# A transformer block in float32r halves: matmul tiles placed at other offsets within 128 bytes

## The chip, the cores and the metric

One NeuronCore of a Trainium2 chip runs the whole program in one launch. The metric is the device time of that core in microseconds (us). The engines named below are TensorE (PE; its loads of the stationary operand are listed apart, as PEld), VectorE (DVE), ScalarE (ACT), GpSimd (POOL) and SyncE (SP), which issues most transfers.

## What is computed

The reference is one block over 256 tokens of width 2048: a modulated norm, a mixer (three attention branches beside a gated linear recurrence), a second modulated norm, and a layer of 16384 small experts, 16 picked for each of 8 heads. Cut to what matters here:

```python
mod = jax.nn.silu(c) @ ada_w + ada_b                    # six vectors of 2048
h = rms_norm(x, norm_mix_g) * (1 + sc1) + sh1
x = x + gt1 * hybrid_mixer(h, w_in, w_out, ...)         # z = h @ w_in ; ... ; y @ w_out
h = rms_norm(x, norm_ffn_g) * (1 + sc2) + sh2
q = h @ peer_wq                                         # scores, top 16 of each head -> e, g
act = gelu(einsum('td,thkd->thk', h, down[e])) * g
x = x + gt2 * einsum('thk,thkd->td', act, up[e])
```

The kernel does the expert layer densely: all of `down` times the tokens, gelu, a gate that is zero for experts that were not picked, then all of `up`.

## The kernel before

Every large product runs in three matmuls. A float32 operand is split into two float32r halves, `h` (high) and `l` (the rest): ScalarE casts the high half and VectorE subtracts it from the source (`split`, L197 and L198). Then `mm3` issues high times high (L346), token high times weight low (L347) and token low times weight high (L348) into the same sums. The stationary operand is a slice of 128 token columns; the moving operand is 512 columns of weights. `mm_sub` does this for the two chunks of 128 rows in one part of the stream and for both halves of the tokens (`tb`), so one part costs 12 matmuls, in the order L346, L347, L348, again and again.

Weights come as one stream. SyncE loads 1 MB raw tiles (`raw`, four buffers); `next_part` takes 1024 columns of one at a time, splits it into a buffer `wh` and a buffer `wl`, and `get` hands the pair to the matmuls. There are three buffers of each in the pool `wp`; among the first 52 parts, two of each five use two more in the pool `xp`. The tokens are `xH` and `xL` (16 KB a partition each), written three times: after the first norm, by the mixer's output, after the second norm. In the last stage the tokens' place is taken by the gated activations `ah` and `al` (four buffers each).

The stages, by the names of the sums that the matmuls write: `f`, `a`, `r`, `xg` (the mixer's input projections, to about 350 us, mixed with attention and recurrence), `y` (output projection), `wq` (queries of the experts), then `d` (expert blocks down) and `u` (up). The first 14 `d` blocks run from 480 to 960 us beside the search and the gate build; then six rounds of `u` alone; then two `u` blocks and one `d` block in turn to about 2020 us; then the last `u` blocks. A block of `d` is 96 of these matmuls, a block of `u` is 48.

The allocator puts every tile at a multiple of 32 bytes. Within 128 bytes, the built program of before has `xH` and `xL` at 64, `wh` and `wl` of the pool `wp` at 32, those of the pool `xp` at 96, `ah` and `al` at 32. All slices of these tiles start at multiples of 512 bytes from the tile's start, so each tile's offset holds for all its slices.

Of the kernel before, what the change touches and what calls it, by code (L numbers as in the profile page):

```python
# [15 lines left out]
P = 128  # L16
D = 2048
S = 256
# [47 lines left out]
def kernel(  # L66
# [48 lines left out]
    cs = cp.tile([P, NDC], F32, name="cs")  # L115
    xH = cp.tile([P, NDC, S], F32R, name="xH")
    xL = cp.tile([P, NDC, S], F32R, name="xL")
    ident = con[:, C_ID:C_ID + P]
# [8 lines left out]

# [1 line left out]
    items = []  # L129
# [47 lines left out]
    def load(most=RAWB):  # L177
        """Loads the stream ahead, as far as the rings allow."""
        while pos["load"] < len(items):
            it = items[pos["load"]]  # L180
            if len(raws) >= most:
                return
            t = wp.tile([P, D], F32, tag="raw", bufs=RAWB, name="raw")
            if it[0] == "ada":
                nc.sync.dma_start(t, ada_w[ada_w.shape[0] - NDC + it[1]])
            elif it[0] == "adp":
                nc.sync.dma_start(t, ada_p[it[1]])
            elif it[0] == "cmp":
                nc.sync.dma_start(t, cmp_w[it[1]][:, it[2] * D:(it[2] + 1) * D])
            else:  # L190
                n = it[2] * it[3]
                nc.sync.dma_start(t[:, 0:n], it[1])
            raws.append(t)
            pos["load"] += 1
# [5 lines left out]
    def ada_load():  # L200
        """Loads ahead, as far as the rings allow."""
        n = pos["adl"]
        if n < ada_w.shape[0] - NDC:
            own = n >= 2 * NDC or n < ADO and n % (ADAB + ADA1) < ADAB
            if sum(o == own for o, _ in avs) < (ADAB if own else ADA1):
                if own:
                    t = vp.tile([P, D], F32, tag="av", bufs=ADAB, name="av")
                else:
                    t = xp.tile([P, D], F32, tag="av1", bufs=ADA1, name="av1")
                nc.sync.dma_start(t, ada_w[n])  # L210
                avs.append((own, t))
                pos["adl"] += 1
                return True
        return False

    def ada(m):
        """One chunk of a modulation vector: rows of the turned weights times the conditioning."""
        t = avs.pop(0)[1]
# [5 lines left out]
    def ada_close(seg, k, n):  # L224
        """The biases; where it scales, one plus it, times the norm's gain."""
        m = mod[:, seg, k:k + n]
# [7 lines left out]
    def bg(r):  # L234
        """A share r of a chunk of the modulation vectors that VectorE makes beside the rest."""
        bgn[1] += r
# [13 lines left out]
    def adp_item():  # L250
        """A chunk of the rows of one modulation vector, in four column groups of the array."""
        i = items[pos["take"]][1]
# [9 lines left out]
        if k == NDC - 1:  # L262
            seg = PSEG[i // NDC]
            rw = wp.tile([P, 512], F32, tag="adr", bufs=1, name="adr")
            A.copy(rw, adp.pop("ps"))
# [7 lines left out]
    def next_part():  # L273
        """Emits the next part of the stream; False at its end."""
        if pos["take"] >= (pos["end"] or len(items)):
# [16 lines left out]
        pool, tag, bufs = (xp, "1", 2) if pos["n"] <= XPN and pos["n"] % 5 >= 3 else (wp, "", AHEAD + 1)  # L292
        wh = pool.tile([P, 2, 512], F32R, tag="wh" + tag, bufs=bufs, name="wh")
        wl = pool.tile([P, 2, 512], F32R, tag="wl" + tag, bufs=bufs, name="wl")
        fh, fl = wh.rearrange("p k n -> p (k n)"), wl.rearrange("p k n -> p (k n)")
# [18 lines left out]

# [1 line left out]
    jobs = []  # L316
# [13 lines left out]

    # steps per part of the stream, by the kind of work; the gate build's first steps go as fast as they may
    tk, wn = [0.0], [0]
# [7 lines left out]
    def finish(prio):  # L340
        """Runs the jobs up to that priority to their end."""
        while jobs and jobs[0][0] <= prio:
            step()
# [25 lines left out]
    def rsqrt(pool, ss, n, w, name, parts=P, bufs=2):  # L369
        """1/sqrt(ss/n + eps) of a few columns, by Newton's method from an integer first guess."""  # L370
        v = pool.tile([parts, w], F32, tag="rsv", bufs=bufs, name=f"rsv_{name}")
# [45 lines left out]

# [1 line left out]
    ea, e0, eq = ExitStack(), ExitStack(), ExitStack()  # L419
# [40 lines left out]
    def ada_first(n):  # L460
        """Chunks of the first two modulation vectors; the tokens' next two chunks when they are complete."""
        for _ in range(n):
# [10 lines left out]

    # two sets of four blocks, in turn over pieces of the width; the sums of the set that rests wait in SBUF
    sums = {"f": [], "a": []}
# [36 lines left out]
    def rest(b, name):  # L512
        """The rest of one of the first four blocks, added up in SBUF."""
        pst = [ps_x(f"{name}_{tb}") for tb in range(NT)]
# [17 lines left out]
    def mix(*gens, rate=0.0):  # L532
        """Steps of several pieces of work in turn."""
        gens = list(gens)
# [7 lines left out]

# [1 line left out]
    ap = ea.enter_context(tc.tile_pool(name="ap", bufs=1))  # L544
# [18 lines left out]
    vc = zp.tile([16, NG, HD], F32, name="vc")  # L563
    # the compressed branch borrows what the later branches fill
    win = oT.rearrange("p h t -> p (h t)").rearrange("p (a l g n) -> p a l g n", a=2, l=32, g=2)
# [3 lines left out]
    def table(i):  # L569
        """The rotation's tables with a norm's gains folded in."""  # L570
        gv = row[:, P * i:P * i + P]
# [8 lines left out]
    def rope(dst, src, nh, cos, sin, name):  # L580
        """dst = src*cos + swap(src)*sin over nh heads of 128."""
        b = tp1.tile([P, nh, 2, 64], F32, tag="ropeb", bufs=1, name=f"rb_{name}")
# [126 lines left out]

# [1 line left out]
    lw = rn.tile([P, 2, RB, P], F32, name="lw")  # L711
    G.dma_start(lw, lru_w)
    def recurrence(gr):
        n = RG
        if True:
# [4 lines left out]
            for c_ in range(n):  # L720
# [13 lines left out]
                A.activation(ta[:, c_], ta[:, c_], AF.Tanh, scale=spl[:, k:k + 1], bias=spl[:, k:k + 1])  # L734
            # d = 1/(1 + tanh) refined from (1 + exp)/2; decay 2d - 1; input sqrt(tanh) d (1 + ti) u
            d = xr[:, :, 0:S]
# [16 lines left out]

# [1 line left out]
    held = {}  # L755

    def scores(sp, g, tb):
        """Unnormed weights of the causal and the windowed branch, and their sums."""
        n = (tb + 1) * P
# [28 lines left out]
    def outputs(sp, g, tb):  # L788
        """The compressed branch's weights; all gated weights turned and times the values."""
        hs = slice(4 * g, 4 * g + 4)  # L790
# [56 lines left out]

# [1 line left out]
    def norm_stats(pool, rbs, o, name, pre=None):  # L849
# [174 lines left out]

# [1 line left out]
    ssr = yp.tile([P, NT], F32, name="ssr")  # L1026
# [22 lines left out]

# [1 line left out]
    bp = ctx.enter_context(tc.tile_pool(name="bp", bufs=1))  # L1051
# [19 lines left out]
    def ev_wq(j, pst):  # L1071
        """Scores of two heads; leaves them to the search."""
        res = []
# [19 lines left out]
    def search(j, tb, sc):  # L1093
        for k in range(4):
            top16(mv[:, tb, 4 * j + k], mi[:, tb, 4 * j + k], sc[:, k * P:(k + 1) * P], P, f"a{j}{tb}{k}")
            yield
        # both lists are sorted: rank (a, b) has (a + 1)(b + 1) - 1 before it, so only those under 16 can be picked
        cd = kq.tile([P, 2, NCD], F32, tag="cd", bufs=2, name=f"cd{j}{tb}")
# [14 lines left out]
    def picks(tb):  # L1113
        """From places in the candidate lists to expert rows, and the softmax; heads and picks on partitions."""
        hi = kq.tile([P, 2, PH, TOPK], U32, tag="hi", bufs=1, name=f"hi{tb}")
# [3 lines left out]
        V.tensor_copy(mf, mi[:, tb])  # L1119
        # place p of rank (a, b): a = max(p / 8 - 1, p / 4 - 6, 0), b = p - min(16 a, 8 a + 8, 4 a + 24)  # L1120
        V.tensor_scalar(hi[:, 0], pk[:, tb], 3, None, OP.logical_shift_right)
# [39 lines left out]
    def w_build():  # L1161
        """Gate weights by expert and token: per token the product of two one-hot tables."""
        stg, ohs, gas, wps = {}, {}, {}, {}
# [27 lines left out]

# [1 line left out]
    xTt, wts, actH, actL = {}, {}, {}, {}  # L1193
# [31 lines left out]
    def act(eb, pool):  # L1225
        t, w = xTt.pop(eb), wts.pop(eb)
        t4 = t.rearrange("p c (g t) -> p c g t", g=8)
        h = pool.tile([P, 4, S], F32R, tag="ah", bufs=4, name=f"ah{eb}")
        l = pool.tile([P, 4, S], F32R, tag="al", bufs=4, name=f"al{eb}")
# [182 lines left out]
```

## Time and profile before

| | before |
|---|---|
| median of 3 runs | 2092.45 us (2089.61 to 2093.78) |
| profiled execution: span from first to last instruction | 2090.6 us |
| mean granted TensorE clock in it | 0.986 of full speed |
| PE / PEld / DVE / ACT busy | 97% / 78% / 69% / 50% |
| instructions in the span | 24862 |
| HBM rate over the span | 243 GB/s |

The span lies inside the spread of the runs: what lies around it is smaller than the spread from run to run. Busy time of PE is the time in which at least one matmul is in the array; matmuls overlap, so it says that PE is hardly ever empty, and not how fast it goes. The page's mean of one matmul is from its start to the end of its drain, longer than the time from one start to the next, which I call the pitch.

### The profile page before, as it was taken

How to read it: one execution, taken by the hardware profiler on the slowest of the kernel's cores; microseconds unless marked ns; L12 is line 12 of the kernel's file. 1: busy time of each engine (PE TensorE's matmuls, PEld its weight loads, DVE VectorE, ACT ScalarE, POOL GpSimd, SP SyncE). 2: the span in 40 equal slices, each digit the busy share in tenths (PEclk: the TensorE clock that was granted, in tenths of full speed). 3: DMA queues.
4: the chain of work that ended last, by engine and by line, in shares of the span. 5: the costliest groups of instructions: out<-in, count | busy, mean ns of one | idle time of the engine just before them, and what ended most of it. 6: DMA issues, size and time to landing. Idle time of an engine off the chain costs nothing.

```text
span 2090.6 us, 24862 instructions
## 1 busy us (share of the span) xinstructions
PE 2025.0 (97%) x9434; PEld 1635.6 (78%) x9434; DVE 1449.4 (69%) x2149; ACT 1053.0 (50%) x1526; POOL 60.9 (3%) x95
## 2 busy tenths in 40 slices
PE   5999997999999999999999999999999999999998
PEld 4777664877888888887888888888888888888887
DVE  7888999887998666646667766665555555555566
ACT  3544676545456777854444444444444444444443
POOL 0000000000000000001000000000000000000000
PEclk8999998999999999999999999999999999999999
DMA  9897788994556666579777877765555565555563
GB/s 374 333 358 310 264 341 312 347 347 165 174 177 201 226 218 241 203 258 332 253 243 258 294 251 253 247 244 191 191 193 200 200 202 194 200 201 191 194 209 141
DMA packets 75849, 508.73 MB, mean 243 GB/s; under 512 B 8528, under 2 KB 9040, under 8 KB 20176
## 3 DMA queue, kind: packets, MB, share of 16 engines
q1 hardware_dynamic: 63792, 450.50, 60.5%
q0 software_dynamic: 11936, 56.63, 7.6%
q8 instruction: 74, 1.21, 0.2%
q14 instruction: 47, 0.39, 0.1%
HBM read 478.78 MB, written 28.31 MB: 243 GB/s over the span
## 4 chain that ended last, share of the span: by engine, by line
PE 86%; DVE 6%; issue 3%; DMA 3%; ACT 1%; POOL 0%; SPq 0%; DVEq 0%; POOLq 0%; ACTq 0%
PE d L348 11%; PE d L346 11%; PE d L347 11%; PE u L347 10%; PE u L348 10%; PE u L346 10%; PE w L1184 3%; DVE av L219 2%; DVE wl L198 2%; PE wq L346 1%; PE wq L347 1%; PE wq L348 1%; PE a L347 1%; PE a L348 1%; PE a L346 1%
## 5 line engine op out<-in xcount | busy, mean ns | idle before, releaser
L198 DVE TENSOR_TENSOR wl<-raw,wh 128x1024 fp32r<-128x1024 f32 x649 | 789.6, 1222 | 511.8 <-ACT wh L197 511.6
L197 ACT CAST wh<-raw 128x1024 fp32r<-128x1024 f32 x649 | 680.0, 1050 | 777.8 <-PE u L348 334.5
L346 PE MATMUL d<-wh,xH 128*128 128x512 f32 x1024 | 411.2, 402 | 0.0
L347 PE MATMUL d<-wl,xH 128*128 128x512 f32 x1024 | 405.1, 396 | 0.9 <-DVE wl L198 0.9
L348 PE MATMUL d<-wh,xL 128*128 128x512 f32 x1024 | 404.9, 395 | 0.0
L346 PE MATMUL u<-wh,ah 128*128 128x512 f32 x1024 | 402.1, 393 | 0.0
L347 PE MATMUL u<-wl,ah 128*128 128x512 f32 x1024 | 399.4, 390 | 1.3 <-DVE wl L198 1.2
L348 PE MATMUL u<-wh,al 128*128 128x512 f32 x1024 | 399.1, 390 | 0.0
L348 PEld LDWEIGHTS d<-wh,xL 128*128 128x128 f32 x1024 | 192.4, 188 | 45.8
L347 PEld LDWEIGHTS d<-wl,xH 128*128 128x128 f32 x1024 | 192.7, 188 | 43.9 <-DVE wl L198 1.3
L346 PEld LDWEIGHTS d<-wh,xH 128*128 128x128 f32 x1024 | 192.8, 188 | 42.6
L347 PEld LDWEIGHTS u<-wl,ah 128*128 128x128 f32 x1024 | 192.4, 188 | 41.8 <-DVE wl L198 3.0
L348 PEld LDWEIGHTS u<-wh,al 128*128 128x128 f32 x1024 | 192.2, 188 | 40.5
L346 PEld LDWEIGHTS u<-wh,ah 128*128 128x128 f32 x1024 | 192.3, 188 | 39.0
L219 DVE SCALAR_TENSOR_TENSOR av<-av,cb 128x2048 f32<-128x2048 f32 x64 | 146.0, 2285 | 5.4 <-DMA av<-in_ada_w_dram 5.4
L1168 DVE TENSOR_TENSOR oh<-con,idT 128x1024 f32<-128x1024 f32 x64 | 78.3, 1223 | 64.2 <-PE w L1184 64.2
L1189 ACT ACTIVATE oh<-oh,gT 128x128 f32<-128x128 f32 x256 | 83.7, 394 | 34.8 <-DVE oh L1168 34.5
L1256 DVE TENSOR_TENSOR acc<-acc,u 128x512 f32<-128x512 f32 x112 | 71.6, 681 | 0.0
L1184 PEld LDWEIGHTS w<-oh 128*128 128x128 f32 x512 | 65.5, 191 | 4.4
L1184 PE MATMUL w<-oh 128*128 128x128 f32 x512 | 66.6, 275 | 0.0
L346 PE MATMUL y<-wh,xH 128*128 128x512 f32 x128 | 52.1, 409 | 3.6 <-ACT xH L197 3.6
L346 PE MATMUL wq<-wh,xH 128*128 128x512 f32 x128 | 52.5, 410 | 2.5 <-ACT xH L197 2.5
(365 smaller groups left out, 2044.8 us busy)
## 6 DMA issues: line engine op xcount, KB each, us to landing
raw<-in_down_dram SPq DMA_DIRECT2D x128, 1024.0 KB, 5.0
raw<-in_up_dram SPq DMA_DIRECT2D x128, 1024.0 KB, 5.0
av<-in_ada_w_dram SPq DMA_DIRECT2D x64, 1024.0 KB, 7.1
raw<-in_w_a_dram SPq DMA_DIRECT2D x32, 1024.0 KB, 9.4
raw<-in_ada_p_dram SPq DMA_DIRECT2D x16, 1024.0 KB, 7.1
raw<-in_w_out_dram SPq DMA_DIRECT2D x16, 1024.0 KB, 7.9
raw<-in_wq_dram SPq DMA_DIRECT2D x16, 1024.0 KB, 5.0
wd<-stg POOLq DMA_DIRECT2D x8, 2048.0 KB, 8.0
```

Of the source, the lines that this page charges most:

```text
L197: A.copy(dst_h, src)
L198: V.tensor_tensor(dst_l, src, dst_h.bitcast(F32), OP.subtract)
L219: V.scalar_tensor_tensor(out=t, in0=t, scalar=1.0, in1=cb, op0=OP.mult, op1=OP.mult, accum_out=m)
L346: T.matmul(o, ah, bh, start=first, stop=False)
L347: T.matmul(o, ah, bl, start=False, stop=False)
L348: T.matmul(o, al, bh, start=False, stop=last)
L1168: V.tensor_tensor(oh, iota.unsqueeze(1).unsqueeze(1).to_broadcast([P, 4, 2, P]), idT[:, 4 * q:4 * q + 4].unsqueeze(3).to_broadcast([P, 4, ...
L1184: T.matmul(wps[p_][:, k * P:(k + 1) * P], oh[:, k, 1], oh[:, k, 0], start=True, stop=True)
L1189: A.activation(ohs[p_][:, k, 0], ohs[p_][:, k, 0], AF.Copy, scale=gT[:, t:t + 1])
L1256: V.tensor_tensor(a, a, pst[tb], OP.add)
```

## The change

`shifted` allocates a tile 32 elements (128 bytes) longer and uses it from 8 elements (32 bytes) times `by` on. It is applied to `xH` (by 3), `xL` (by 2), `ah` (by 1), and to each weight buffer by a count of the parts: `wh` by the count modulo 4, `wl` by the count divided by 4, modulo 4. `al` stays. The tile `adr` of 2 KB, used once, is now a buffer of the ring `zr` (two buffers), which makes room.

```diff
+    def shifted(pool, n, by, **kw):
+        return pool.tile([P, n + 32], F32R, **kw)[:, 8 * by:8 * by + n]
-    xH = cp.tile([P, NDC, S], F32R, name="xH")
-    xL = cp.tile([P, NDC, S], F32R, name="xL")
+    xH = shifted(cp, NDC * S, 3, name="xH").rearrange("p (k t) -> p k t", t=S)
+    xL = shifted(cp, NDC * S, 2, name="xL").rearrange("p (k t) -> p k t", t=S)
...
-            rw = wp.tile([P, 512], F32, tag="adr", bufs=1, name="adr")
+            rw = zrow(adpool[0], "adr")
...
-        wh = pool.tile([P, 2, 512], F32R, tag="wh" + tag, bufs=bufs, name="wh")
-        wl = pool.tile([P, 2, 512], F32R, tag="wl" + tag, bufs=bufs, name="wl")
+        turn = pos["n"] % 16
+        wh = shifted(pool, 1024, turn % 4, tag="wh" + tag, bufs=bufs, name="wh").rearrange("p (k n) -> p k n", k=2)
+        wl = shifted(pool, 1024, turn // 4, tag="wl" + tag, bufs=bufs, name="wl").rearrange("p (k n) -> p k n", k=2)
...
-        h = pool.tile([P, 4, S], F32R, tag="ah", bufs=4, name=f"ah{eb}")
+        h = shifted(pool, 4 * S, 1, tag="ah", bufs=4, name=f"ah{eb}").rearrange("p (k t) -> p k t", t=S)
```

Row by row, every engine has the same instructions in the same order before and after; only the name of the tile `adr` differs in two rows. The other tiles move by multiples of 128 bytes. With the base addresses of the built program of after, the offsets within 128 bytes become:

| tile | before | after |
|---|---|---|
| `xH` | 64 | 32 |
| `xL` | 64 | 0 |
| `ah` | 32 | 64 |
| `al` | 32 | 32 |
| `wh` (pool `wp`) | 32 | 32, 64, 96, 0 from part to part |
| `wl` (pool `wp`) | 32 | 32, 64, 96, 0, changing every four parts |

## Rows read from the trace of the kernel before

**Rows 1.** The page: busy time by engine, and the chain that ended last.
```profile
PE 2025.0 (97%) x9434; PEld 1635.6 (78%) x9434; DVE 1449.4 (69%) x2149; ACT 1053.0 (50%) x1526; POOL 60.9 (3%) x95
...
PE 86%; DVE 6%; issue 3%; DMA 3%; ACT 1%; POOL 0%; SPq 0%; DVEq 0%; POOLq 0%; ACTq 0%
```
**Rows 2.** Windows: busy PE, PEld, DVE, ACT, POOL (instructions); clock, DMA share, GB/s.
```profile
480.00:960.00 480.00, 479.13 (x2432) 399.83 (x2431) 343.00 (x694) 309.88 (x560) 18.01 (x31) 1.00 0.60 213
1160.00:2020.00 860.00, 859.07 (x3809) 701.14 (x3808) 500.10 (x511) 377.31 (x398) 16.32 (x20) 1.00 0.63 214
```
**Rows 3.** The page's costliest groups: matmuls of d and u, by operand.
```profile
L346 PE MATMUL d<-wh,xH 128*128 128x512 f32 x1024 | 411.2, 402 | 0.0
L347 PE MATMUL d<-wl,xH 128*128 128x512 f32 x1024 | 405.1, 396 | 0.9 <-DVE wl L198 0.9
...
L346 PE MATMUL u<-wh,ah 128*128 128x512 f32 x1024 | 402.1, 393 | 0.0
L347 PE MATMUL u<-wl,ah 128*128 128x512 f32 x1024 | 399.4, 390 | 1.3 <-DVE wl L198 1.2
...
L346 PE MATMUL wq<-wh,xH 128*128 128x512 f32 x128 | 52.5, 410 | 2.5 <-ACT xH L197 2.5
L346 PE MATMUL y<-wh,xH 128*128 128x512 f32 x128 | 52.1, 409 | 3.6 <-ACT xH L197 3.6
```
**Rows 4.** Timeline of PE (start us, us): ends of one undisturbed block of d.
```profile
1226.33 0.40 PE L348 MATMUL u<-wh,al 128*128 128x512 f32 x1
1226.57 0.39 PE L346 MATMUL d<-wh,xH 128*128 128x512 f32 x1
...
1248.96 0.39 PE L346 MATMUL u<-wh,ah 128*128 128x512 f32 x1
```
**Rows 5.** Stretch of u alone; only instructions of u; PE, PEld, DVE, ACT, clock.
```profile
1000.00:1150.00 150.00, 150.00 (x664) 124.19 (x663) 17.10 (x27) 0.00 (x0) 1.00 0.73 250
```
**Rows 6.** Timeline of PE: a part of u after four transposes.
```profile
1618.20 0.40 PE L347 MATMUL u<-wl,ah 128*128 128x512 f32 x1
...
1620.29 0.39 PE L347 MATMUL u<-wl,ah 128*128 128x512 f32 x1
```
**Rows 7.** Timeline of PE: a part of d after matmuls of the gate build.
```profile
689.37 0.40 PE L347 MATMUL d<-wl,xH 128*128 128x512 f32 x1
...
691.46 0.40 PE L347 MATMUL d<-wl,xH 128*128 128x512 f32 x1
```
**Rows 8.** Three us early in wq, after an idle stretch: clock, then timeline.
```profile
477.00:480.00 3.00, 3.00 (x8) 0.50 0.00 0
...
477.34 0.63 PE L347 MATMUL wq<-wl,xH 128*128 128x512 f32 x1
477.76 0.63 PE L346 MATMUL wq<-wh,xH 128*128 128x512 f32 x1
```
**Rows 9.** The recurrence's plain float32 matmuls: all (min/median/max ns), then seven in a row.
```profile
L730 PE MATMUL rp<-u,lw x32: 377/379/763, 245.5 to 333.1; 128*128 128x256 f32 x32
...
245.55 1.67 PE L730 MATMUL rp<-u,lw 128*128 128x256 f32 x7
```
**Rows 10.** Timeline of PE: first and last of 41 gate-logit matmuls in a row.
```profile
264.38 0.28 PE L346 MATMUL gl<-xH,wh 128*24 128x256 f32 x1
...
268.96 0.28 PE L347 MATMUL gl<-xL,wh 128*24 128x256 f32 x1
```
**Rows 11.** VectorE's subtraction (min/median/max ns), 40 to 160 us, then 960 to 2080 us.
```profile
L198 DVE TENSOR_TENSOR wl<-raw,wh x38: 1214/1220/1226, 44.1 to 154.6; 128x1024 fp32r<-128x1024 f32 x38
...
L198 DVE TENSOR_TENSOR wl<-raw,wh x399: 1216/1225/1227, 960.6 to 2077.7; 128x1024 fp32r<-128x1024 f32 x200
```
**Rows 12.** Timeline: the copy into adr, its four transposes, the next use of zr.
```profile
350.29 0.59 ACT L265 COPY adr<-adp 128x512 f32<-128x512 f32 x1 [0.82 <-PE adp L259]
...
351.20 0.60 PE L268 MATMUL adt<-con,adr 128*128 128x128 f32 x4
...
353.01 0.59 ACT L703 COPY zr_r<-xg 128x512 f32<-128x512 f32 x1 [2.13 <-PE xg L348]
```

## The prediction, made before the changed kernel ran

> **What bounds the kernel now.** I read the page first: PE is busy 97% of the span and holds 86% of the chain that ended last [rows 1]. Then I cut the span into stretches, because an average over stages says little. From 480 to 960 us PE has work for 479.13 of 480.00 us, from 1160 to 2020 us for 859.07 of 860.00 us, at full granted clock, while VectorE and ScalarE have room (500.10 and 377.31 us of the second stretch) and the transfers take 0.63 of the DMA engines [rows 2]. Two thirds of the kernel are therefore a queue of matmuls, and the time there is their number times their pitch, the time from one start to the next.
>
> The page's durations include the drain, so the reader should not take 402 ns for the cost of one. But they differ: matmuls of `d` last 402 and 396 ns, those of `u` 393 and 390 ns [rows 3], with the same shape, type and number. The timeline gives the pitch. A block of `d` starts at 1226.57 us and the first matmul behind its 96 starts at 1248.96 us: 22.39 / 96 = 233.2 ns [rows 4]. In 150 us of `u` alone, 664 matmuls touch the stretch, two of them as overlap at its start: 150 / 662 = 226.6 ns [rows 5]. What differs between the two is the stationary tile alone: `xH` and `xL` at offset 64, `ah` and `al` at 32, against weights at 32 in both. So the tile's place does matter, by some 6.6 ns a matmul, and it matters through the load that runs beside the moving operand: the last matmul of `u` before a block of `d` still has its own operands at 32 and 32, but the load of `xH` runs beside it, and it takes 1226.57 - 1226.33 = 0.24 us [rows 4].
>
> Two more views size what a better place could give. At half clock (granted 0.50), the same matmuls start 477.76 - 477.34 = 0.42 us apart [rows 8]. Plain float32 matmuls of 256 columns at full clock: seven in 1.67 us, the last with its drain of 0.379, so (1.67 - 0.379) / 6 = 215 ns [rows 9]. Half the pitch at half clock, 210 ns at this view's resolution, and this 215 agree; I take 216 ns as the floor of one such matmul at full clock (an estimate from these two rows). Over it `u` pays about 11 ns and `d` about 17. That is the whole stake: 17 ns times all matmuls paced by PE.
>
> **How a distance acts.** I describe a matmul by the distance, within 128 bytes, from the stationary tile loaded beside it to its weights. Before, it is 0 in all of `u` and 32 in all of the rest (32 one way for buffers of `wp`, the other way for those of `xp`, where the mixer's stages, mixed with other work, show no clean run to compare). A distance of 64 does not occur in a full matmul. The second thing that the timeline shows is that 226.6 is a settled state. After four transposes a part of `u` takes nine pitches from 1618.20 to 1620.29 us, 2.09 / 9 = 232.2 ns, although all its offsets are 32 [rows 6]. In `d` after an interruption nine pitches also take 691.46 - 689.37 = 2.09 us, 232.2 ns [rows 7]. Out of the settled state both distances cost the same; `u` gains its 5.6 ns by running long in one unchanged pattern.
>
> **The change part by part.** Instructions, their order, the queues and the transfers are the same, so nothing is added or moved on any engine. The costs are in four places.
>
> The adr tile: its ring neighbour `zr` is next written at 353.01 us, while the transposes that read adr end at 351.20 + 0.60 = 351.80 us [rows 12]. 1.2 us of cover, cost nothing; without cover it would be one copy of 0.59 us.
>
> Writes and reads of the shifted tiles by VectorE and ScalarE: VectorE's subtraction lasts 1220 ns (median) between 40 and 160 us, where two of five buffers lie at offset 96, and 1225 ns later, where all lie at 32, with minimum and maximum 12 ns apart at most [rows 11]. The offset costs them nothing. Were it 5 ns each, 649 of them would be 3 us of VectorE, hidden in its free 31% [rows 1].
>
> Matmuls that now lie at distance 32: `d`, `wq` and `y` have 3 x (1024 + 128 + 128) = 3840 that PE paces [rows 3]; a quarter of them go to each of the distances 0, 32, 64 and 32 the other way, since `wh` and `wl` walk through four offsets while `xH` and `xL` stand still. From part to part, every 12 matmuls, the distance changes, and inside a part L347 has another distance than L346 and L348. I therefore expect no settled state, and give each known distance the unsettled 232.2 ns.
>
> Matmuls now at distance 0: the 3072 of `u` [rows 3] lose their single pattern and also see all four distances. The remaining 864 (`f`, `a`, `r`, `xg`) share their stages with other work and are taken as unchanged; 1 ns on each would be 0.9 us.
>
> The unknown is X, the pitch at distance 64. From below, it cannot pass the floor of 216. From above, I continue the line of 226.6 at distance 0 and 233.2 at 32 to about 240 at 64 (an estimate from [rows 4, 5]). A mixture is in the trace: the gate logits run with all four distances in turn, 40 pitches from 264.38 to 268.96 us, 114.5 ns for 256 columns [rows 10]; doubled this is 229 ns, but their loads are 24 columns, not 128, so it is a low reading. Between 216 and 240 I take X equal to the unsettled 232.2, the row that full matmuls are nearest to. Then all distances cost 232.2:
> 3840 x (232.2 - 233.2) = -3.8 us; 3072 x (232.2 - 226.6) = +17.2 us; sum +13.4 us. The profiled span of 2090.6 would be 2104.0; the median of the runs lies 1.9 above that span, so 2092.45 + 13.4 = 2105.9, **2106 us**.
>
> A rule that speaks against any effect stands in the Trainium skill, page "TensorE: Matmul & The Clock Gate", Part 2, step 1: the array has separate read ports for the moving operand and for LDWEIGHTS, and loading the next weights "doesn't steal SBUF read bandwidth from the running matmul". By it the sum is 0 and the time 2092; this trace disagrees with it as far as `d` and `u` differ by 6.6 ns with nothing but the stationary tile exchanged [rows 4, 5].
>
> **The rivals.**
> *Faster: distance 64 is free of collisions.* If two streams collide by their place in 128 bytes, the farthest distance could reach the floor. With X = 216 the mean is (3 x 232.2 + 216) / 4 = 228.1: 3840 x -5.1 = -19.6, 3072 x +1.5 = +4.6, together -15 us, 2077 us. It decides at a mean pitch of (3840 x 233.2 + 3072 x 226.6) / 6912 = 230.3: below that the change gains. The 229 of the gate logits speaks for it, their short loads against it. If the changing offsets alone brought every matmul to the floor, it would be 3840 x -17.2 - 3072 x 10.6 = -99 us, 1994 us; nothing in the trace comes near 216 with 128 float32r columns loaded beside, and I give it 3 in 100.
> *Slower by more: distance 64 is worst.* With X = 240 the mean is 234.2: 3840 x 1.0 + 3072 x 7.6 = +27 us, 2119 us. For it speaks that 32 is worse than 0 when settled.
> *No change: the place in 128 bytes is not what makes the difference.* `xH` and `ah` also lie far apart in the partition, and `u` could be quick for that reason; then the shift does nothing, 2092 us. Against it: the unsettled runs show that the pitch of `u` is no property of its buffers.
>
> **How the numbers follow.** Forecast (all distances about 232): 0.40. Distance 64 worst: 0.17. Distance 64 free, or the mixture as quick as the gate logits: 0.27, the floor included. No change: 0.16. A measurement of this kernel cannot tell less than about 0.2%, 4 us, from nothing. Faster by more than that takes the third case with little of the first, 0.28; within 0.2% the fourth, 0.16; slower the first two, 0.56. The forecast's own range is 2098 to 2114; with the faster case at 2077 and the slower at 2119, and some room for X a little above the line, 8 in 10 lie between 2076 and 2124.
>
> **What the profile after would show.** Right: the pitch in `u` alone at about 232 instead of 226.6, with no long run of equal pitches, and a block of `d` at about 22.3 us instead of 22.39; so `u` and `d` move in opposite ways. VectorE's and ScalarE's durations, and the wait before the copy at 353.01 us, stay. In parts, by the count modulo 4, one in four should stand out if X is far from 232: its L346 and L348 are shorter (faster rival) or longer (slower rival). Wrong: `u` keeps 226.6, or `d` falls by more than 3 ns; then distances 0 and 64 average below what unsettled runs show, and my use of [rows 6, 7] as the price of a changing pattern is the step that failed.

## The result, and the profile after

The changed kernel is slower: a median of 2103.77 us (4 runs, 2101.69 to 2104.33) against 2093.11 us (4 runs, 2089.61 to 2094.94) of the kernel before on the same chip, a ratio of 1.0052 with a 95% interval of 1.0038 to 1.0067. The profiled span went from 2090.6 to 2101.5 us, at a mean granted clock of 0.985 after 0.986.

The page's busy times, answering to [rows 1]:

```profile
PE 2035.3 (97%) x9434; PEld 1636.0 (78%) x9434; DVE 1450.1 (69%) x2149; ACT 1051.0 (50%) x1526; POOL 60.9 (3%) x95
```

PE's busy time grew by 10.3 us, almost all of the span's 10.9; VectorE's and ScalarE's changed by 0.7 and -2.0 us. What is left of the span beside it is 66.2 us after 65.6. So no wait was added: the same 9434 matmuls took longer. The windows of the two long stretches, in the columns of [rows 2], say which:

```profile
480.00:960.00 480.00, 479.63 (x2437) 400.75 (x2436) 343.76 (x695) 310.27 (x560) 18.02 (x31) 1.00 0.61 214
1160.00:2020.00 860.00, 859.77 (x3784) 696.94 (x3783) 498.92 (x509) 372.52 (x394) 16.31 (x20) 1.00 0.63 214
```

In 480 us of `d` and the search, 2437 matmuls touch the window where 2432 did. In 860 us of mostly `u`, 3784 where 3809 did. One kind became a little quicker, the other slower. The page's groups agree (busy us, then mean ns of one; [rows 3] are those of before):

```profile
L351 PE MATMUL d<-wh,xH 128*128 128x512 f32 x1024 | 410.9, 401 | 0.0
L351 PE MATMUL u<-wh,ah 128*128 128x512 f32 x1024 | 407.1, 398 | 0.0
L352 PE MATMUL u<-wl,ah 128*128 128x512 f32 x1024 | 404.4, 395 | 0.7 <-DVE wl L202 0.7
L352 PE MATMUL d<-wl,xH 128*128 128x512 f32 x1024 | 403.9, 394 | 0.4 <-DVE wl L202 0.4
```

Matmuls of `u` went from 393 and 390 ns to 398 and 395, those of `d` from 402 and 396 to 401 and 394. The pitch itself needs starts. In the window of `u` alone (only instructions of `u`, as [rows 5]), 648 matmuls touch 150 us instead of 664, so the pitch is 150 / 646 = 232.2 ns instead of 226.6:

```profile
1000.00:1150.00 150.00, 150.00 (x648) 121.40 (x647) 16.62 (x26) 0.00 (x0) 1.00 0.72 242
```

The timeline of the changed kernel, first the place of the tile that was `adr` (answering to [rows 12]), then the ends of an undisturbed block of `d` (answering to [rows 4]):

```profile
350.77 0.59 ACT L269 COPY zr_adr<-adp 128x512 f32<-128x512 f32 x1 [0.82 <-PE adp L263]
...
351.68 0.60 PE L272 MATMUL adt<-con,zr_adr 128*128 128x128 f32 x4
...
353.49 0.59 ACT L708 COPY zr_r<-xg 128x512 f32<-128x512 f32 x1 [2.13 <-PE xg L353]
...
1230.53 0.40 PE L353 MATMUL u<-wh,al 128*128 128x512 f32 x1
1230.76 0.40 PE L351 MATMUL d<-wh,xH 128*128 128x512 f32 x1
...
1253.04 0.39 PE L351 MATMUL u<-wh,ah 128*128 128x512 f32 x1
```

The copy that now shares a ring with `adr` comes 2.13 us after its last wait as before, and still 1.2 us behind the transposes. The block of `d` takes 22.28 / 96 = 232.1 ns a matmul, where it took 233.2.

The mean pitches below, here and further on, are means of the times from one start to the next over a whole run, those over 300 ns (interruptions, and stretches at half clock) left out; the changes are multiplied by the numbers of matmuls.

| | pitch before, ns | after, ns | change, us |
|---|---|---|---|
| `d`, `y`, `wq` (3840) | 233.1 | 231.9 | -4.6 |
| `u` (3072) | 227.3 | 232.3 | +15.4 |
| sum | | | +10.8 |

### The profile page after: what moved, and what is told of

Read it like the earlier page. It is cut to its first block, busy times and chain, and to the rows that moved or that the text cites. A ratio compares the mean times of both kernels' runs of the same rounds, so it can differ in the third digit from the quotient of the medians.

```text
span 2101.5 us, 24861 instructions
## 1 busy us (share of the span) xinstructions
PE 2035.3 (97%) x9434; PEld 1636.0 (78%) x9434; DVE 1450.1 (69%) x2149; ACT 1051.0 (50%) x1526; POOL 60.9 (3%) x95
## 4 chain that ended last, share of the span: by engine, by line
PE 78%; issue 9%; DVE 8%; ACT 2%; DMA 2%; POOL 1%; SPq 0%; DVEq 0%; POOLq 0%; ACTq 0%
PE d L351 11%; PE d L352 11%; PE d L353 11%; PE u L352 8%; PE u L353 8%; PE u L351 8%; DVE av L223 3%; PE w L1189 3%; DVE wl L202 2%; PE wq L351 1%; PE wq L352 1%; PE wq L353 1%; PE y L351 1%; PE y L353 1%; PE y L352 1%
## 5 line engine op out<-in xcount | busy, mean ns | idle before, releaser
L351 PE MATMUL u<-wh,ah 128*128 128x512 f32 x1024 | 407.1, 398 | 0.0
L352 PE MATMUL u<-wl,ah 128*128 128x512 f32 x1024 | 404.4, 395 | 0.7 <-DVE wl L202 0.7
L353 PE MATMUL u<-wh,al 128*128 128x512 f32 x1024 | 404.0, 395 | 0.0
L1189 PEld LDWEIGHTS w<-oh 128*128 128x128 f32 x512 | 65.6, 191 | 4.4
```

The lines of the kernel that those rows point to most:

```text
L351: T.matmul(o, ah, bh, start=first, stop=False)
L352: T.matmul(o, ah, bl, start=False, stop=False)
L353: T.matmul(o, al, bh, start=False, stop=last)
L1189: T.matmul(wps[p_][:, k * P:(k + 1) * P], oh[:, k, 1], oh[:, k, 0], start=True, stop=True)
```

## The experiments

The theory at the start is that of the prediction: a matmul's pitch follows from the distance within 128 bytes between the tile being loaded and the weights being streamed, and an unchanged distance settles. Its rivals stand in the expectations. In the tables, "worked out" is 3840 and 3072 times the changes of that run's mean pitches against 233.1 and 227.3, and "measured" the difference of the medians of kernel and before in the same runs.

**Both parts apart, and constant distances.** Four kernels keep the change's longer tiles and alter the shifts; `al`, which the change leaves as it was, is longer by 128 bytes too.

e1_all_at_0 puts every tile at the same offset within 128 bytes, with no walk:

```diff
-    xL = shifted(cp, NDC * S, 2, name="xL").rearrange("p (k t) -> p k t", t=S)
+    xL = shifted(cp, NDC * S, 3, name="xL").rearrange("p (k t) -> p k t", t=S)
...
-        wh = shifted(pool, 1024, turn % 4, ...
-        wl = shifted(pool, 1024, turn // 4, ...
+        wh = shifted(pool, 1024, 0, ...
+        wl = shifted(pool, 1024, 0, ...
...
-        h = shifted(pool, 4 * S, 1, ...
-        l = pool.tile([P, 4, S], F32R, ...
+        h = shifted(pool, 4 * S, 0, ...
+        l = shifted(pool, 4 * S, 0, ...
```

> Weights at 32 in every part, xH, xL, ah and al at 32 too: distance 0 everywhere, nothing changes from part to part. Theory of the settled pattern (a constant distance 0 settles at 226.6 ns, anything interrupted or changing costs about 232): u as before; the 18 blocks of d behind 960 us fall from 233.2 to 226.6 ns (1728 x 6.6 = 11 us), the 14 interrupted blocks before it gain little; time 2070 to 2082 us. Rival (u was quick because ah lies elsewhere in the partition, not because of its offset): d stays at 233, time 2093 us. Second rival (the price per distance is fixed, settled or not): all 3840 matmuls gain 6.6 ns, 2068 us.

e2_all_at_64 has the same weights, and `xH`, `xL` by 1, `ah`, `al` by 2, so that every distance within 128 bytes is 64:

```diff
+    xH = shifted(cp, NDC * S, 1, ...
+    xL = shifted(cp, NDC * S, 1, ...
...
+        h = shifted(pool, 4 * S, 2, ...
+        l = shifted(pool, 4 * S, 2, ...
```

> Weights at 32 in every part, xH, xL, ah and al at 96: the distance of 64, which no full matmul had before, everywhere and constant. Settled pattern: some settled pitch appears in both d and u, equal in both. If farther is freer (the faster rival of the prediction): near 216 ns, time about 1990 us. If farther is worse: 240 ns, time about 2093 + 3840 x 0.007 + 3072 x 0.013 = 2160 us. If all distances other than 0 settle alike: 233 in both, 2093 + 3072 x 0.0066 = 2113 us. Place in the partition as the cause: no change, 2093 us.

e3_weights_in_turn keeps the walk of the weights and takes the tokens' shifts away:

```diff
+    xH = shifted(cp, NDC * S, 0, ...
+    xL = shifted(cp, NDC * S, 0, ...
...
+        h = shifted(pool, 4 * S, 0, ...
+        l = shifted(pool, 4 * S, 0, ...
```

> Only the weight buffers walk through four offsets; xH, xL stay at 64, ah and al at 32. Settled pattern: the same loss as the whole change, since the walk alone prevents the settled state: u at 232, d at 232, time 2102 to 2107 us. Rival (the fixed offsets of the tokens make the loss): u keeps 226.6 and the time is 2093 us.

e4_tokens_only keeps the tokens' shifts and takes the walk away:

```diff
+        wh = shifted(pool, 1024, 0, ...
+        wl = shifted(pool, 1024, 0, ...
...
+        l = shifted(pool, 4 * S, 0, ...
```

> Only the token tiles move: xH at 32, xL at 0, ah at 64, al at 32; weights stay at 32. Within a group of three matmuls the distances now differ (0, 32, 0 in d; 32 the other way, 0, 32 in u), but the pattern repeats every three matmuls. Settled pattern: both d and u settle again, at a pitch between 226 and 235 ns that the three distances set; time 2080 to 2115 us. Rival (what counts is the share of matmuls at distance 0, settled or not): d has two thirds at 0, 228.8, and u one third, 231: 2093 - 17 + 14 = 2090 us.

| | ratio (95%) | `d`, ns | `u`, ns | worked out, us | measured, us |
|---|---|---|---|---|---|
| e1_all_at_0 | 1.0002 (0.9993 to 1.0011) | 230.6 | 230.8 | +1.2 | +0.1 |
| e2_all_at_64 | 1.0056 (1.0038 to 1.0073) | 232.9 | 231.1 | +10.9 | +9.9 |
| e3_weights_in_turn | 1.0041 (1.0025 to 1.0057) | 231.9 | 231.8 | +9.2 | +9.4 |
| e4_tokens_only | 1.0024 (1.0015 to 1.0033) | 231.3 | 231.7 | +6.6 | +5.0 |

The time is in the pitches: worked out and measured agree within 2 us. e3 came, 0.2 us below its range, as the first theory had it. But e1 fits neither: its time is that of the rival, 2093 us, but by a gain in `d` and a loss in `u` that cancel, and no theory had the loss. Its profile contradicts the first theory: all its offsets are equal within 128 bytes and stay so, and `u` has lost its 226.6, as its window of `u` alone shows (652 touch it, 150 / 650 = 230.8 ns):

```profile
1000.00:1150.00 150.00, 150.00 (x652) 121.98 (x651) 17.89 (x28) 0.00 (x0) 1.00 0.73 248
```

e2 came at none of its four times, and its `d` and `u` are not equal. And e4 has no walk, yet nothing settles: in `u` alone its parts of 12 matmuls have means from 229.1 to 234.2 ns, which come back in the same order every 12 parts. What these share with the change is the 128 bytes of padding: a buffer of 4096 bytes plus 128 puts its neighbour 128 bytes further, modulo 256, so that distances alternate by 128 from buffer to buffer even where no shift is made. With three buffers of weights and four parts to a block of `u`, such a pattern comes back every 12 parts. The second theory is therefore a period of 256 bytes (or more), with the padding as the third thing that the change does.

**Padding, walk, and a constant shift.** f4_padding_only is the change with every shift at 0 (`by` is 0 in all five calls and `al` is padded too):

```diff
+    xH = shifted(cp, NDC * S, 0, ...
+    xL = shifted(cp, NDC * S, 0, ...
...
+        wh = shifted(pool, 1024, 0, ...
+        wl = shifted(pool, 1024, 0, ...
...
+        h = shifted(pool, 4 * S, 0, ...
+        l = shifted(pool, 4 * S, 0, ...
```

> The whole change with every shift set to 0: only the 128 bytes added to each tile are left, the offsets within 128 bytes are those of before. Theory now: the padding alone breaks the settled state, u at 230 to 232 and d at about 232; 2100 to 2107 us, nearly the whole loss. First theory (offsets within 128 bytes): u 226.6, d 233.2, 2093 us.

f6_walk_without_padding starts from before and lets only `wh` of the pool `wp` walk, in buffers that are longer by 512 bytes (here and in all later kernels but f2, `adr` is in the ring as in the change, for room):

```diff
+        if pool is wp:
+            o = 8 * (pos["n"] % 4)
+            wh = wp.tile([P, 1152], F32R, tag="wh", bufs=bufs, name="wh")[:, o:o + 1024].rearrange("p (k n) -> p k n", k=2)
```

> The kernel before, with only wh of the pool wp walking through four offsets, in buffers 512 bytes longer, so that they stay at multiples of 512 bytes; wl does not walk (adr in zr for room). Theory now: inside a part the distances hold, but L347 differs from L346 and L348 in three of four parts; u has a quarter of its parts at 226.6 and the others between 229 and 235, mean 230 to 232; 2097 to 2106 us. If the walk costs nothing by itself and the padding is all: u 226.6, 2093 us.

f1_gap_288 starts from before and puts 288 unused bytes behind `xL`. Modulo 256 that is 32 bytes, which takes `xH` and `xL` from a distance of 224 to the weights of `wp` to 0; `ah` and `al` stay at 0:

```diff
+    gap = cp.tile([P, 72], F32, name="gap")
...
-            rw = wp.tile([P, 512], F32, tag="adr", bufs=1, name="adr")
+            rw = zrow(adpool[0], "adr")
```

> The kernel before with an unused tile of 288 bytes behind xL (adr moved to the ring zr as in the change, for room). No buffer is longer, so all weight buffers stay at multiples of 512 bytes from each other; the distance from xH and xL to the weights goes from 224 to 0 within 512 bytes, as in u. First theory (constant within 128 bytes is enough to settle) was contradicted by the run with all tiles at 32, where nothing settled. Theory now (what must stay constant is the distance within 512 bytes, which buffers 128 bytes longer destroy): the undisturbed d settles at 226.6 ns, u keeps 226.6; 18 blocks x 96 x 6.6 ns = 11 us, with a little from the interrupted blocks 2076 to 2082 us. Rival (the region of the tile in the partition): d stays at 233, 2093 us.

| | ratio (95%) | `d`, ns | `u`, ns | worked out, us | measured, us |
|---|---|---|---|---|---|
| f4_padding_only | 1.0025 (1.0016 to 1.0035) | 231.8 | 230.8 | +5.8 | +6.2 |
| f6_walk_without_padding | 1.0043 (1.0027 to 1.0058) | 232.5 | 231.5 | +10.6 | +8.7 |
| f1_gap_288 | 0.9906 (0.9887 to 0.9926) | 227.6 | 227.2 | -21.4 | -19.2 |

Padding alone costs 6 us, the walk of one buffer alone 9, the whole change 10.7. They don't add up: `u` loses 3.5, 4.2 and 5.0 ns in the three, so either part takes most of what there is to lose. f4 came a little below the 2100 us expected at least; its `u` has the same distances modulo 256 as that of e1, and the same mean, 230.8. f6 came as expected, f1 3 us better than its range. In f1, a shift of 32 bytes modulo 256 gives all of `d` the pitch of `u`: its undisturbed block takes 21.76 / 96 = 226.7 ns in the timeline,

```profile
1262.63 0.39 PE L347 MATMUL d<-wh,xH 128*128 128x512 f32 x1
...
1284.39 0.39 PE L347 MATMUL u<-wh,ah 128*128 128x512 f32 x1
```

and in its page's groups `d` and `u` now differ by 4 ns for `wh`, where it was 9, and by nothing for `wl`, where it was 6:

```profile
L347 PE MATMUL d<-wh,xH 128*128 128x512 f32 x1024 | 406.8, 397 | 0.0
L347 PE MATMUL u<-wh,ah 128*128 128x512 f32 x1024 | 402.3, 393 | 0.0
L348 PE MATMUL u<-wl,ah 128*128 128x512 f32 x1024 | 399.4, 390 | 1.8 <-DVE wl L199 1.7
L348 PE MATMUL d<-wl,xH 128*128 128x512 f32 x1024 | 399.8, 390 | 0.5 <-DVE wl L199 0.4
```

The weights, `ah` and `al` all lie 32 bytes further modulo 256 in f1 than before, and `u` keeps its pitch (227.2 after 227.3): by this move it is the distance between the tiles that counts, and not the place of each.

**The period.** f2_sweep_u moves `ah` and `al` of each round (192 matmuls, four blocks of `u`) 32 bytes further than in the round before, from 0 to 480 (buffers longer by 512 bytes):

```diff
+        o = 8 * (eb // 2)
+        h = pool.tile([P, 4 * S + 128], F32R, tag="ah", bufs=4, name=f"ah{eb}")[:, o:o + 4 * S].rearrange("p (k t) -> p k t", t=S)
+        l = pool.tile([P, 4 * S + 128], F32R, tag="al", bufs=4, name=f"al{eb}")[:, o:o + 4 * S].rearrange("p (k t) -> p k t", t=S)
```

> The kernel before, with ah and al of round g of the last stage 32 bytes times g from their tile's start (tiles 512 bytes longer, so at multiples of 512 bytes): each round of u has one constant distance, from 0 to 480 within 512 bytes in 16 steps. Theory now: each round settles at a pitch of its own; round 0 226.6, the round with the distance of d (224) 233.3, the others between the floor of 216 and 240. If the period is 128 bytes, rounds 0, 4, 8, 12 are alike, if 256, rounds 0 and 8. d stays at 233.2.

It ran once, for its pitches and not its time (2101.19 us). Moving `ah` and `al` on by 32 takes 32 bytes off the distance from them to the weights. The first matmuls of rounds 1 to 5 in its timeline lie 192 matmuls apart: 44.79 us or 233.3 ns, then 233.3, 234.2 and 233.2 ns. Inside the first three of these rounds, groups of 24 pitches stay within 0.7 ns of each other; the fourth (a shift of 128) runs at 233.3 up to an interruption in its middle and at 232.1 to 232.7 behind it.

```profile
1003.02 0.39 PE L346 MATMUL u<-wh,ah 128*128 128x512 f32 x1
...
1047.81 0.40 PE L346 MATMUL u<-wh,ah 128*128 128x512 f32 x1
...
1092.61 0.39 PE L346 MATMUL u<-wh,ah 128*128 128x512 f32 x1
...
1137.58 0.40 PE L346 MATMUL u<-wh,ah 128*128 128x512 f32 x1
...
1182.36 0.40 PE L346 MATMUL u<-wh,ah 128*128 128x512 f32 x1
```

Mean pitch in ns by the shift of `ah` and `al`, in bytes:

| shift | 0 | 32 | 64 | 96 | 128 | 160 | 192 | 224 |
|---|---|---|---|---|---|---|---|---|
| from 0 | 227.3 | 233.3 | 233.3 | 234.2 | 232.8 | 233.3 | 229.1 | 233.2 |
| from 256 | 227.6 | 233.2 | 233.4 | 234.0 | 232.3 | 233.4 | 229.1 | 233.3 |

The second row repeats the first within 0.5 ns: the period is 256 bytes. Half of it, 128, is no good place, which is what e1 and f4 ran into. It is not symmetric: 64 bytes one way cost 233.3, the other way (a shift of 192) 229.1. Without interruption a constant distance does settle, but at a pitch of its own, from 227 to 234. In the six rounds of `u` alone nothing changes but `ah` and `al`, so it is the place of the loaded tile that moves the pitch.

**How exact the match must be, and for whom.** Both kernels start from f1 with the `ah` and `al` of f2; g1_fine_sweep_u moves them in steps of 4 bytes through the match, g3_one_operand moves only one of the two at a time.

```diff
+        g = eb // 2
+        oh, ol = 56 + g, 56 + g
```

> The kernel with the gap of 288 bytes, with ah and al of round g at a distance of 32 - 4 g bytes, from 32 to -28, constant in a round. The sweep in steps of 32 showed a period of 256 bytes, 227.1 to 227.6 ns at 0 and 256, 229.1 at 64, 232 to 234 elsewhere. If the chip looks at lines of 16 or 32 bytes, rounds in the same line are alike, with steps at multiples of 16 or 32; if the match at 0 is an exact one, only round 8 settles at 226.7 and its neighbours lie near 230 or above. A lower pitch than 226.7 near 0 would make a better version than 2073 us.

```diff
+        g = eb // 2
+        oh, ol = 8 * g if g < 8 else 0, 0 if g < 8 else 8 * (g - 7)
```

> The kernel with the gap of 288 bytes; in rounds 1 to 7 of the last stage only ah (read in two of three matmuls) moves by 32 bytes times g, in rounds 8 to 15 only al (one of three) by 32 to 256. If each matmul paid for its own distance, rounds 1 to 7 would lie two thirds of the way from 226.7 to the sweep's pitch of that distance (231.1 at 32, 228.3 at 64) and rounds 8 to 14 one third (228.9, 227.5). If the pattern as a whole settles or not, one moved operand costs nearly as much as both: 231 to 234. Round 15 is at 256 and should be 227 again.

One run each (2091.22 and 2092.62 us). In g1 the rounds 4, 8, 12, 16 and 32 bytes to one side of the match have means of 231.7, 233.3, 233.3, 228.6 and 233.3 ns, on the other side 232.5, 230.7, 229.3 and 229.2 for the first four, and 235.0 at 28 bytes; the match itself has 227.4, and no round is below it. In g3, with `ah` alone moved, means are 229.4 to 233.5; with `al` alone, which only every third matmul loads, 230.8 to 233.3; with neither, 226.8 to 227.8. At the same shift, one operand in three costs about three fifths or more of what all cost, where a price for each matmul by itself would be one third; so what is lost belongs to the whole sequence of matmuls and not to the matmul with the bad distance.

The round 12 bytes off shows more, in g1's timeline:

```profile
1701.56 0.39 PE L347 MATMUL u<-wh,ah 128*128 128x512 f32 x1
...
1706.77 0.39 PE L349 MATMUL u<-wh,al 128*128 128x512 f32 x1
1707.00 0.60 PE L1208 MATMUL xt<-con,ge 128*128 128x128 f32 x4
...
1714.32 0.40 PE L348 MATMUL u<-wl,ah 128*128 128x512 f32 x1
...
1719.84 0.40 PE L348 MATMUL u<-wl,ah 128*128 128x512 f32 x1
```

Coming from a settled block of `d`, its first 23 pitches are 5.21 / 23 = 226.5 ns, although the distance is wrong. Then four transposes interrupt, four more do so 12 matmuls on, and the same operands go on at 5.52 / 24 = 230.0 ns (236 and 224 ns in turn) up to the next block of `d`. The round 16 bytes off on the same side does this only in its second half:

```profile
1802.72 0.39 PE L347 MATMUL u<-wh,ah 128*128 128x512 f32 x1
...
1813.38 0.39 PE L349 MATMUL u<-wh,al 128*128 128x512 f32 x1
...
1847.30 0.40 PE L347 MATMUL u<-wh,ah 128*128 128x512 f32 x1
...
1858.26 0.39 PE L349 MATMUL u<-wh,al 128*128 128x512 f32 x1
```

Both stretches lie behind two such interruptions and have the same distance, but the first runs at 10.66 / 47 = 226.8 ns and the second at 10.96 / 47 = 233.2. At the match, the pitch was back at 226.7 four and six pitches behind the second interruption of the round's two halves. So a distance doesn't fix the pitch: as far as these rounds show, it limits which patterns can hold, and what ran before decides which of them does.

**A forecast of either sign.** If the period is 256 and the match is the place that returns to 226.7, then weights that walk by 256 must lose nothing, and one wrong constant distance for all must be slower than the change. h1_walk_by_256 (a gap of 32 bytes instead of f1's 288):

```diff
+    gap = cp.tile([P, 8], F32, name="gap")
...
+        if pool is wp:
+            o = 64 * (pos["n"] % 2)
+            wh = wp.tile([P, 1152], F32R, tag="wh", bufs=bufs, name="wh")[:, o:o + 1024].rearrange("p (k n) -> p k n", k=2)
```

> The kernel with a gap behind xL, now 32 bytes (distance 256 from the tokens to the weights), and wh of the pool wp 256 bytes further in every second part, in buffers 512 bytes longer. The walk of the change in steps of the period that the sweep showed. If only the distance within 256 bytes counts: u and the undisturbed d settle at 226.7 ns as with the gap of 288, 2071 to 2076 us. If any change of place from part to part unsettles: 231 to 232, about 2100 us.

h2_all_at_160 (the worst place of f2, a shift of 96 or a distance of 160 from tokens to weights; for `d` by a gap of 448 bytes, for `u` by an offset of 96):

```diff
+    gap = cp.tile([P, 112], F32, name="gap")
...
+        h = pool.tile([P, 4 * S + 128], F32R, tag="ah", bufs=4, name=f"ah{eb}")[:, 24:24 + 4 * S].rearrange("p (k t) -> p k t", t=S)
+        l = pool.tile([P, 4 * S + 128], F32R, tag="al", bufs=4, name=f"al{eb}")[:, 24:24 + 4 * S].rearrange("p (k t) -> p k t", t=S)
```

> The kernel with the gap, now 448 bytes, and ah and al 96 bytes from their tile's start (tiles 512 bytes longer): distance 160 within 256 bytes everywhere and constant, the worst step of the sweep (234.0 to 234.2 ns). Against the gap of 288: u 3008 x (234.1 - 227.1) = 21 us, undisturbed d 1728 x (234.1 - 226.7) = 13 us, interrupted d and wq and y about 2000 x 5.5 = 11 us: 2113 to 2121 us. If a constant distance settles to a gain whatever it is: below 2093 us.

| | ratio (95%) | `d`, ns | `u`, ns | worked out, us | measured, us |
|---|---|---|---|---|---|
| h1_walk_by_256 | 0.9911 (0.9886 to 0.9935) | 227.6 | 227.1 | -21.7 | -21.2 |
| h2_all_at_160 | 1.0116 (1.0099 to 1.0133) | 234.1 | 234.3 | +25.3 | +23.0 |

Both came as expected. The timelines of an undisturbed block of `d`, first h1 with 21.77 / 96 = 226.8 ns,

```profile
1215.74 0.39 PE L351 MATMUL d<-wh,xH 128*128 128x512 f32 x1
...
1237.51 0.39 PE L351 MATMUL u<-wh,ah 128*128 128x512 f32 x1
```

then h2 with 22.49 / 96 = 234.3 ns:

```profile
1235.12 0.39 PE L347 MATMUL d<-wh,xH 128*128 128x512 f32 x1
...
1257.61 0.40 PE L347 MATMUL u<-wh,ah 128*128 128x512 f32 x1
```

Same instructions, same clock of 1.00 in these stretches, 44 us between their medians (2072.18 and 2116.37 us), by addresses alone. f1 and h1 beat both kernels of this study, at 2073.20 and 2072.18 us.

## Why the prediction was right, and where it was not

The forecast was 2106 us, slower by 13.4; measured were 2103.77, slower by 10.7. Step by step:

- **The bound** was PE's queue of matmuls: PE's busy time took 10.3 of the span's 10.9 us.
- **`u` loses its settled state**, priced +17.2, measured +15.4. The pitch after is 232.3, as taken from [rows 6]. The term was too large by 1.8 us, by its other end: 226.6 is the pitch of undisturbed `u`, while its mean over the kernel, with the stretches after interruptions that [rows 6] show, was 227.3.
- **`d`, `wq` and `y` gain a little**, priced -3.8, measured -4.6 (231.9 against 232.2).
- **The tile `adr`, VectorE and ScalarE at nothing**: the copy's wait is the same 2.13 us, and the median of VectorE's subtraction late in the run is 1226 ns, where it was 1225.
- **X, the pitch at distance 64**, taken as 232.2: sorted by distance within 128 bytes, the matmuls of `d` and `u` in after have means of 231.5 to 233.1, those at 64 231.5 and 232.1. No part by the count modulo 4 stands out. Both rivals that hung on X, 216 and 240, are out; but with a period of 256 bytes each of these classes mixes two distances, so X was no one quantity.
- **The rival of no change**, by the place of whole tiles, is out by f1: 288 bytes of gap took 5.5 ns from the mean pitch of `d` and left `u` as it was.

The mechanism that decided the result was right: `u` had a quick settled pattern, and the change took it away. What failed is the description under the forecast. "Distance within 128 bytes" has half the true period, the line 226.6, 233.2, 240 has no basis (f2 has 233.3 at a shift of 64, 234 at 96, and 229.1 at 192), and "unsettled" is not a state with a price: constant distances settle too, at 229 to 235. The forecast survived because walk and padding run through several such patterns, whose mixture lies near the 232 that [rows 6, 7] showed for disturbed ones; that the two agree was luck, since nothing in the rows said that they must. It also missed the third part of the change: the padding, which it took for room alone, costs 6 us by itself (f4). And its own rows, 226.6 ns where the distance is 0 and 233.2 where it is 32, already pointed to what f1 shows: 32 bytes in the right place are worth 19 us.

The rule of the Trainium skill that the prediction weighed (page "TensorE: Matmul & The Clock Gate", Part 2, step 1, that a load beside a matmul takes no read bandwidth from it) would leave the loaded tile's place without effect. Here it has one: 227.3 against 234.2 ns in f2 with only `ah` and `al` moved, and 226.8 against 234.3 ns in h1 and h2 with nothing but addresses exchanged; whether read bandwidth is what is lost, no run shows. What inside the chip has the period of 256 bytes stays open, as does why 226.7 was found again in both halves of the round at the match and in one half 16 bytes off, and why even it stays 11 ns above the estimated floor of 216. A matmul without a load beside it was not tried.

## What to carry to other kernels

Where matmuls of this kind follow each other without a gap, place the loaded and the streamed tiles at the same offset modulo 256 bytes, in every buffer of a ring, and pad by multiples of 256, never by 128. Judge it by the time from one start to the next in an undisturbed stretch: PE's busy share was 97% in the best and in the slower kernel alike. Before a place is varied, read the distances from the built program, since an unused tile of 32 bytes moves everything behind it.

## What was not expected of the hardware

- The period of 256 bytes in the distance between the stationary tile loaded beside a matmul and its moving tile: 226.7 ns at the match; with the stationary tile further on by 32 to 224 bytes 232 to 234 ns, but 229 at 192.
- Four bytes off the match are enough to lose it (means of 231.7 and 232.5 ns): on one side the round ran at 226.7 from a settled block of `d` up to the first transposes, and at 233.3 behind them.
- The pitch has a memory: 12 bytes off the match the same operands ran at 226.5 ns before an interruption and at 230.0 behind it, and 16 bytes off at 226.8 behind one pair of interruptions and at 233.2 behind another.
- One mismatched operand in three slows the whole sequence to 230.8 to 233.3 ns.
